# Weight pools kept open through all stages of a decoder trunk, and weight-block sums made by accumulating DMAs

## The chip, the cores and the metric

The kernel runs on one core of a Trainium2 chip. The core has five engines with in-order instruction queues of their own: TensorE (PE) for matmuls, VectorE (DVE), ScalarE (ACT), GpSimd (POOL) and SyncE (SP); PE also loads its stationary operand (PEld), which overlaps the matmuls. SP issues most DMAs, and POOL can issue them too; all of them run on the core's 16 DMA engines. Data live in HBM, in SBUF (128 partitions) and, for matmul results, in PSUM. The metric is the device time of one execution in microseconds (us); less is better.

## The reference

Two residual layers over 256 tokens of width 2048, in float32. Cut to what matters here:

```python
for layer in range(DEPTH):                                  # DEPTH = 2
    h = _rmsnorm(x, mix_norm_g[layer])
    if layer % 2 == 0:                                      # attention (8 heads) and a pooling mixer
        x = x + jnp.concatenate([a, b], axis=-1) @ even_w_out[e]
    else:                                                   # gated short convolution
        x = x + _short_conv(h, odd_w_in[o], odd_conv_w[o], odd_w_out[o])
    x = x + _mlp(_rmsnorm(x, mlp_norm_g[layer]), w_mlp_up[layer], w_mlp_down[layer])

def _mlp(h, w_up, w_down):                                  # 2048 -> 8192 -> 2048
    return jnp.square(jax.nn.relu(h @ w_up)) @ w_down
```

The weights are some 380 MB of float32, each read once per execution; the two MLPs hold most of them. The tokens are few, so nearly all of the work is weights passing through PE.

## The kernel before, in words

**Exactness.** PE multiplies in a reduced float32 form, so each operand is split: a high part `hi` (ACT casts it, line 140) and a low part `lo` (DVE subtracts, line 141). `halved` (line 131) does this for a weight tile of 1 MiB in two pieces, and each tile then gives PE two or three matmuls per block: `columns_out` (lines 157 to 161) where the weights are stationary, `tokens_out` (lines 146 to 155) where the tokens are, and `product` (lines 761 to 767) for blocks of the seven-product scheme below. A "tile" below is one such 1 MiB of weights, and its "preparation" the four instructions of `halved`.

**Weight pools.** `slab` (line 122) takes a buffer of the pool `raws`, issues its load on SP and calls `halved`, which takes buffers of the pool `halves` (six `hi` and six `lo`, three tiles' worth). `new_stage` (line 77) closes the pools of the stage that ends and opens new ones; it is called for the latents (line 213), after them (line 389), at the start of each MLP (line 715) and at the start of the convolution (line 898). In an MLP `raws` has two buffers and a pool `blocks` three, elsewhere `raws` has three.

**An MLP.** The hidden width 8192 is cut in 16 chunks of 512, and chunks go in eight pairs. `up_chunk(c)` makes one chunk's hidden values from four weight tiles (in four steps) and two steps of squaring and splitting. The product with `w_down` covers a pair's 1024 rows and 2048 columns in four column blocks of 512. Blocks 2 and 3 are done by `down_block`, two tiles each. For the first seven pairs blocks 0 and 1 are done by `down_seven` (line 750): the two token halves, the two column blocks and the pair's even and odd row groups make a 2 x 2 by 2 x 2 block product, which Strassen's scheme in Winograd's form does in seven products instead of eight. The token side of it (`sum_forms`, line 742) is made once per chunk. The weight side needs sums of the four blocks b11, b12, b21, b22 (rows even or odd, column block 0 or 1): DVE makes b12 - b11, b12 + b22, b22 + b11's new value and b21 - b22's new value, each in one instruction over 128 x 2048 elements (lines 787 and 790, called at 803, 812, 813 and 825). A running sum per product (`totals`) is kept over the pairs, and combined at the last of the seven. The last pair does all four blocks by `down_block`. The loop at lines 871 to 883 interleaves steps of `down_seven`, `up_chunk` and `down_block`.

**The order of the work.** A scheduler sorts each engine's instructions by its own estimate of when each could start; what waits for what is then kept by semaphores. So a change of the buffers can move instructions on engines that it does not name. At a stage's end the residual `x` gets its last column block (lines 858, 671 or 674, DVE), ACT squares it for the norm (`squares`, line 289), PE transposes it (`turn_block`, line 297) and ACT and DVE write the transposed block to `xT` (lines 204, 205). Since `xT` is filled block by block, the next stage's matmuls can begin before its last block is there.

## Time and profile before

| | us |
|---|---|
| median of 3 runs | 2035.02 |
| lowest and highest of them | 2035.01 and 2038.82 |
| the profiled execution's own time | 2038.12 |
| its span, first to last instruction | 2036.3 |
| PE busy | 2013.3 (99% of the span) |
| DVE busy | 1503.7 (74%) |
| ACT busy | 1115.8 (55%) |
| POOL busy | 52.5 (3%) |
| mean granted TensorE clock, share of 2.4 GHz | 0.997 |

PE's busy time is 99% of the span, so what is not PE's work is some 23 us in all. The chain of waits names the work that ended last, step by step; the waits of PE name each idle stretch and what ended it. The table of windows gives each engine's busy time in a stretch, the granted clock of TensorE as a share of 2.4 GHz, the mean busy share of the 16 DMA engines, and the rate at which they moved data. Matmuls are pipelined, so that the durations of single ones overlap, and what one costs is better taken from the chain's share divided by the count.

### The profile page before, as it was taken

The page shows a single profiled execution, that of the slowest core. Times are in us where ns is not written, and L with a number is a line of the kernel's source. Part 1 is how long each engine was busy: PE and PEld are TensorE (multiplying, and loading weights), DVE is VectorE, ACT ScalarE, POOL GpSimd, SP SyncE. Part 2 cuts the span into 40 slices and gives each one's busy share as a digit, 9 for nine tenths or more (in the row PEclk, how much of TensorE's full clock was granted, in tenths as well). Part 3 has the DMA queues.
Part 4 walks back from the last instruction along what each step waited for, and adds up shares of the span by engine and source line. Part 5 has one row for each costly group of instructions (what it writes and reads, how often), then busy time and mean ns, then how long its engine had stood idle before and what let it go on. Part 6 is the DMA issues. An engine that isn't in the chain of part 4 may idle for free.

```text
span 2036.3 us, 26507 instructions
## 1 busy us (share of the span) xinstructions
PE 2013.3 (99%) x10534; PEld 1726.1 (85%) x10534; DVE 1503.7 (74%) x1795; ACT 1115.8 (55%) x1480; POOL 52.5 (3%) x76
## 2 busy tenths in 40 slices
PE   8999999999999999999999999999999999999999
PEld 7987888888888888888788888888888888888887
DVE  5767559797887978875566656559797787978874
ACT  5457447565555655555444444546665556655552
POOL 2240000000000000000000000000000000000000
PEclk9999999999999999999999999999999999999999
DMA  7555365755757557555555555466665756657454
GB/s 243 160 173 182 128 197 178 225 176 191 230 165 231 166 187 227 166 182 183 173 186 186 186 186 187 164 216 197 196 200 171 241 167 203 206 166 239 154 186 145
DMA packets 195820, 384.20 MB, mean 189 GB/s; under 512 B 6224, under 2 KB 16336, under 8 KB 195696
## 3 DMA queue, kind: packets, MB, share of 16 engines
q1 hardware_dynamic: 195312, 382.23, 57.8%
q8 instruction: 82, 1.34, 0.3%
q0 software_dynamic: 352, 0.27, 0.1%
q14 instruction: 42, 0.34, 0.1%
q10 hardware_dynamic: 32, 0.01, 0.0%
HBM read 380.39 MB, written 2.10 MB: 188 GB/s over the span
## 4 chain that ended last, share of the span: by engine, by line
PE 97%; DMA 1%; ACT 1%; DVE 1%; issue 0%; SPq 0%; POOL 0%; DVEq 0%; ACTq 0%
PE ps L160 32%; PE ps L161 16%; PE ps L153 10%; PE ps L155 10%; PE ps L154 10%; PE ps L765 4%; PE ps L767 4%; PE ps L766 4%; PE ps L166 1%; PE ps L168 1%; PE ps L167 1%; DMA raw<-in_even_w_in 1%; PE ps L297 1%; ACT hi L140 0%; DVE lo L141 0%; PE ps L614 0%
## 5 line engine op out<-in xcount | busy, mean ns | idle before, releaser
L160 PE MATMUL ps<-xT,hi 128*128 128x512 f32 x2816 | 993.3, 395 | 3.3 <-ACT hi L140 3.3
L141 DVE TENSOR_TENSOR lo<-raw,hi 128x1024 fp32r<-128x1024 f32 (+2 forms) x610 | 739.3, 1226 | 331.5 <-ACT hi L140 327.9
L140 ACT CAST hi<-raw 128x1024 fp32r<-128x1024 f32 (+2 forms) x610 | 633.2, 1049 | 508.4 <-PE ps L160 206.5
L161 PE MATMUL ps<-xT,lo 128*128 128x256 f32 x2816 | 791.1, 281 | 0.2
L160 PEld LDWEIGHTS ps<-xT,hi 128*128 128x128 f32 x2816 | 530.5, 188 | 126.6 <-ACT hi L140 3.7
L161 PEld LDWEIGHTS ps<-xT,lo 128*128 128x128 f32 x2816 | 529.2, 188 | 5.3 <-DVE lo L141 1.4
L153 PE MATMUL ps<-hi,hT 128*128 128x512 f32 (+1 forms) x896 | 349.1, 390 | 0.0
L155 PE MATMUL ps<-hi,hT 128*128 128x512 f32 (+1 forms) x896 | 347.3, 388 | 0.0
L154 PE MATMUL ps<-lo,hT 128*128 128x512 f32 (+1 forms) x896 | 347.2, 387 | 0.0
L140 ACT CAST hi<-b 128x1024 fp32r<-128x1024 f32 x196 | 204.5, 1051 | 207.8 <-PE ps L160 161.6
L141 DVE TENSOR_TENSOR lo<-b,hi 128x1024 fp32r<-128x1024 f32 x196 | 237.6, 1220 | 44.9 <-ACT hi L140 44.6
L153 PEld LDWEIGHTS ps<-hi,hT 128*128 128x128 f32 x896 | 168.3, 188 | 35.0 <-issue 1.3
L155 PEld LDWEIGHTS ps<-hi,hT 128*128 128x128 f32 x896 | 168.3, 188 | 34.8
L154 PEld LDWEIGHTS ps<-lo,hT 128*128 128x128 f32 x896 | 168.3, 188 | 33.6 <-DVE lo L141 0.4
L765 PE MATMUL ps<-hi,fT 128*128 128x512 f32 x224 | 88.1, 393 | 0.0
L767 PE MATMUL ps<-hi,fT 128*128 128x512 f32 x224 | 87.7, 391 | 0.0
L766 PE MATMUL ps<-lo,fT 128*128 128x512 f32 x224 | 87.1, 389 | 0.0
L194 ACT COPY t<-ps 128x512 f32<-128x512 f32 x88 | 50.8, 578 | 53.6 <-PE ps L161 53.6
L858 DVE SCALAR_TENSOR_TENSOR x<-ps,r,x 128x512 f32<-128x512 f32 (+1 forms) x73 | 52.0, 739 | 19.3 <-PE ps L155 19.3
L765 PE MATMUL ps<-hi,hT 128*128 128x512 f32 x168 | 65.8, 392 | 0.2 <-ACT hT L200 0.2
L767 PE MATMUL ps<-hi,hT 128*128 128x512 f32 x168 | 65.6, 391 | 0.0
L766 PE MATMUL ps<-lo,hT 128*128 128x512 f32 x168 | 65.3, 389 | 0.0
(184 smaller groups left out, 1578.2 us busy)
## 6 DMA issues: line engine op xcount, KB each, us to landing
raw<-in_w_mlp_up SPq DMA_DIRECT2D x128, 1024.0 KB, 5.4
raw<-in_w_mlp_down SPq DMA_DIRECT2D x72, 1024.0 KB, 5.1
b<-in_w_mlp_down SPq DMA_DIRECT2D x56, 1024.0 KB, 6.0
raw<-in_odd_w_in SPq DMA_DIRECT2D x48, 1024.0 KB, 5.2
raw<-in_even_w_out SPq DMA_DIRECT2D x16, 1024.0 KB, 5.2
raw<-in_odd_w_out SPq DMA_DIRECT2D x16, 1024.0 KB, 5.3
raw<-in_even_w_in SPq DMA_DIRECT2D x8, 1024.0 KB, 5.7
raw<-in_even_w_in SPq DMA_DIRECT2D x7, 1088.0 KB, 6.5
```

The source lines that it names most:

```text
L140: a = nc.scalar.copy(h, r)
L141: v = nc.vector.tensor_tensor(out=l, in0=r, in1=h.bitcast(F32), op=ALU.subtract)
L153: nc.tensor.matmul(o, lhsT=a_hi, rhs=hi[:, c0:c0 + n], start=first, stop=False)
L154: nc.tensor.matmul(o, lhsT=a_hi, rhs=lo[:, c0:c0 + n], start=False, stop=False)
L155: nc.tensor.matmul(o, lhsT=a_lo, rhs=hi[:, c0:c0 + n], start=False, stop=last)
L160: nc.tensor.matmul(o, lhsT=hi[:, c0:c0 + P], rhs=act[:, kt, :], start=first, stop=False)
L161: nc.tensor.matmul(o[:, S:2 * S], lhsT=lo[:, c0:c0 + P], rhs=act[:, kt, 0:S], start=False, stop=last)
L194: nc.scalar.copy(t, ps[:, :, S:2 * S])
L765: nc.tensor.matmul(o, lhsT=a_hi, rhs=hi, start=q == 0, stop=False)
L766: nc.tensor.matmul(o, lhsT=a_hi, rhs=lo, start=False, stop=False)
L767: nc.tensor.matmul(o, lhsT=a_lo, rhs=hi, start=False, stop=q == 3)
L858: nc.vector.scalar_tensor_tensor(out=xb, in0=ps[:, t, :n], scalar=r2[0][:, t:t + 1], in1=xb, op0=ALU.mult, op1=ALU.add)
```

## The change

`new_stage` is split in two. With a value for `raw_bufs` it works as before. Without one it closes and opens only the pools named in `more`, and leaves `raws` and `halves` open: `raws` then keeps the three buffers it was given after the latents through both MLPs and the convolution. In an MLP `blocks` has one buffer of each of two tags, `t` and `v`.

`down_seven` no longer calls DVE for the weight side. The signs are chosen so that the four sums need additions alone (column block 0 enters with a negative sign, which the totals take back at the end): `t` is loaded with b12, b11 is added to it, later b22, later b21; `v` is loaded with b12 and b22 is added. Each addition is a DMA from HBM that accumulates into the SBUF tile, issued on POOL (`add`). Blocks b11, b22 and b21, which are used as they are, are loaded into `raws`. So a pair has five plain loads for its seven products where it had four, and four accumulating ones where it had four DVE instructions.

```diff
@@ -74,15 +74,16 @@
     big = ctx.enter_context(tc.tile_pool(name="big", bufs=1))
     stage = []
 
-    def new_stage(raw_bufs, **more):
-
-        for s_ in stage:
+    def new_stage(raw_bufs=0, **more):
+
+        for s_ in reversed(stage[1 - bool(raw_bufs):]):
             s_.close()
-        st = ExitStack()
-        stage[:] = [st]
-        pools.clear()
-        for name, bufs in dict(raws=raw_bufs, halves=6, **more).items():
-            pools[name] = st.enter_context(tc.tile_pool(name=uid(name), bufs=bufs, reuse_waits="tile"))
+        del stage[1 - bool(raw_bufs):]
+        for wanted in (dict(raws=raw_bufs, halves=6) if raw_bufs else {}, more):
+            if wanted:
+                stage.append(ExitStack())
+                for name, bufs in wanted.items():
+                    pools[name] = stage[-1].enter_context(tc.tile_pool(name=uid(name), bufs=bufs, reuse_waits="tile"))
 
     pools = {}
     small = ctx.enter_context(tc.tile_pool(name="small", bufs=2))
...
@@ -712,7 +713,7 @@
         up, down = w_up[layer], w_down[layer]
         hid, sums, totals = {}, {}, {}
         r2 = []
-        new_stage(2, blocks=3, forms=2)
+        new_stage(blocks=1, forms=2)
         pairs = DFF // NB // 2
 
         def up_chunk(c):
@@ -753,10 +754,16 @@
 
             rows_ = down[2 * pair * NB:2 * (pair + 1) * NB].rearrange("(q e p) n -> e p q n", e=2, p=P)
 
-            def block(e, n):
-                b = pools["blocks"].tile([P, 4, NB], F32, tag="b", name=uid("b"))
-                nc.sync.dma_start(b, rows_[e][:, :, n * NB:(n + 1) * NB])
+            def at(e, n):
+                return rows_[e][:, :, n * NB:(n + 1) * NB]
+
+            def block(e, n, tag="raw"):
+                b = pools["raws" if tag == "raw" else "blocks"].tile([P, 4, NB], F32, tag=tag, name=uid(tag))
+                nc.sync.dma_start(b, at(e, n))
                 return b
+
+            def add(b, e, n):
+                nc.gpsimd.dma_start(b, at(e, n), accum_op=ALU.add)
 
             def product(o, b, left):
 
@@ -795,46 +802,45 @@
 
             yield
             b11 = block(0, 0)
+            t = block(0, 1, "t")
+            add(t, 0, 0)
             one = bank2()
             product(one[:, 0, :], b11, own(0, 0))
             summed("p1", one[:, 0, :])
             yield
-            b12 = block(0, 1)
-            minus(b11, b12, b11)
-            product(one[:, 1, :], b11, form(1))
+            v = block(0, 1, "v")
+            add(v, 1, 1)
+            product(one[:, 1, :], t, form(1))
+            add(t, 1, 1)
             summed("p5", one[:, 1, :])
             yield
-            b22 = block(1, 1)
             two = bank2()
-            product(two[:, 0, :], b22, form(3))
+            product(two[:, 0, :], block(1, 1), form(3))
             onto(0, 1, two[:, 0, :])
             yield
-            plus(b12, b22, b12)
-            plus(b22, b22, b11)
-            product(two[:, 1, :], b22, form(2))
-            summed("p6", two[:, 1, :])
+            product(two[:, 1, :], v, form(0))
+            summed("p7", two[:, 1, :])
             yield
             three = bank2()
-            product(three[:, 0, :], b12, form(0))
-            summed("p7", three[:, 0, :])
+            product(three[:, 0, :], t, form(2))
+            add(t, 1, 0)
+            summed("p6", three[:, 0, :])
             yield
-            b21 = block(1, 0)
-            product(three[:, 1, :], b21, own(0, 1))
+            product(three[:, 1, :], block(1, 0), own(0, 1))
             onto(0, 0, three[:, 1, :])
             yield
-            minus(b22, b21, b22)
             four = bank2()
-            product(four[:, 0, :], b22, own(1, 1))
+            product(four[:, 0, :], t, own(1, 1))
             onto(1, 0, four[:, 0, :])
             if pair == pairs - 2:
                 onto(0, 0, totals["p1"])
-                plus(totals["p6"], totals["p6"], totals["p1"])
-                plus(totals["p7"], totals["p7"], totals["p6"])
-                onto(1, 0, totals["p7"])
-                plus(totals["p6"], totals["p6"], totals["p5"])
+                minus(totals["p1"], totals["p1"], totals["p6"])
+                minus(totals["p6"], totals["p5"], totals["p1"])
                 onto(0, 1, totals["p6"])
-                plus(totals["p7"], totals["p7"], totals["p5"])
-                onto(1, 1, totals["p7"])
+                minus(totals["p1"], totals["p1"], totals["p7"])
+                onto(1, 0, totals["p1"])
+                minus(totals["p5"], totals["p5"], totals["p1"])
+                onto(1, 1, totals["p5"])
 
         def down_block(pair, b, last):
 
@@ -895,7 +901,7 @@
     ss, xT = next_norm[0]
 
 
-    new_stage(3, conv=2)
+    new_stage(conv=2)
     conv_pool = pools["conv"]
     R1 = []
     yT = []
```

What the scheduler makes of it is seen in three places. The first is ACT's queue at the end of the first MLP and the start of the convolution; `hi<-raw_8452` in the kernel before and `hi<-raw_8450` in the changed one are the two halves of the convolution's first weight tile (`odd_w_in`), the `junk` rows the squares of a block of `x`, and the last `junk` pair is that of the last block. Before:

```order
L140 CAST hi_8403<-raw_8401 128x1024
L140 CAST hi_8407<-raw_8401 128x1024
L204 ACTIVATE xT_8195<-ps_8288,gains_577 128x256 x4
L289 ACTIVATE junk_8397,ss_8194<-x 128x512
L289 ACTIVATE junk_8399,ss_8194<-x 128x512
L204 ACTIVATE xT_8195<-ps_8380,gains_577 128x256 x4
L289 ACTIVATE junk_8511,ss_8194<-x 128x512
L289 ACTIVATE junk_8513,ss_8194<-x 128x512
L140 CAST hi_8454<-raw_8452 128x1024
L140 CAST hi_8458<-raw_8452 128x1024
```

And now:

```order
L141 CAST hi_8452<-raw_8450 128x1024
L205 ACTIVATE xT_8201<-ps_8294,gains_577 128x256
L141 CAST hi_8456<-raw_8450 128x1024
...
L290 ACTIVATE junk_8403,ss_8200<-x 128x512
L290 ACTIVATE junk_8405,ss_8200<-x 128x512
L141 CAST hi_8515<-raw_8513 128x1024
L141 CAST hi_8519<-raw_8513 128x1024
...
L290 ACTIVATE junk_8509,ss_8200<-x 128x512
L290 ACTIVATE junk_8511,ss_8200<-x 128x512
```

Three tiles of the convolution (6 casts) have moved ahead of the squares of the last block of `x`; before, all of them stood behind.

The second is PE's queue at the end of the attention layer's output projection and the start of the first MLP; `ident,x` are the transposes of the last block of `x`, the `xT,hi` rows the MLP's first tile. Before:

```order
L155 MATMUL ps_2602<-hi_2664,hT_1741 128x512
L160 MATMUL ps_2708<-xT_2333,hi_2712 128x512
L160 MATMUL ps_2709<-xT_2333,hi_2712 128x512
L297 MATMUL ps_2752<-ident,x 128x128 x8
L161 MATMUL ps_2708<-xT_2333,lo_2713 128x256
```

And now:

```order
L156 MATMUL ps_2602<-hi_2664,hT_1741 128x512
L161 MATMUL ps_2700<-xT_2333,hi_2704 128x512
L162 MATMUL ps_2700<-xT_2333,lo_2705 128x256
...
L161 MATMUL ps_2701<-xT_2333,hi_2708 128x512
L162 MATMUL ps_2701<-xT_2333,lo_2709 128x256
L298 MATMUL ps_2744<-ident,x 128x128 x8
```

The transposes stood behind two matmuls of the MLP, and now stand behind 32 (16 of each of the two lines). At the start of the second MLP they have moved back in the same way, by 30 matmuls.

The third is the DMA queues in the middle of the first MLP. SP's loads for one pair now, from the load of `t` on (`raw` with `w_mlp_up` are the tiles of `up_chunk`):

```order
L129 DMA raw_5123<-in_w_mlp_up 128x4x512
L762 DMA t_5270<-in_w_mlp_down 128x4x512
L129 DMA raw_5166<-in_w_mlp_down 128x4x512
L129 DMA raw_5232<-in_w_mlp_down 128x4x512
L762 DMA raw_5268<-in_w_mlp_down 128x4x512
L129 DMA raw_5297<-in_w_mlp_up 128x4x512
...
L129 DMA raw_5559<-in_w_mlp_down 128x4x512
L129 DMA raw_5625<-in_w_mlp_down 128x4x512
L762 DMA v_6050<-in_w_mlp_down 128x4x512
L762 DMA raw_5661<-in_w_mlp_down 128x4x512
```

And the additions on POOL, which had no instruction there before:

```order
L766 DMA t_5270<-in_w_mlp_down 128x4x512 x2
L766 DMA v_6050<-in_w_mlp_down 128x4x512
L766 DMA t_5270<-in_w_mlp_down 128x4x512
L766 DMA t_5981<-in_w_mlp_down 128x4x512 x2
L766 DMA v_6761<-in_w_mlp_down 128x4x512
```

The load of `t` stands three loads ahead of that of its pair's b11 (`raw_5268`), and the load and the addition of the next pair's `v` stand ahead of the third addition to this pair's `t`.

## Rows read from the trace of the kernel before

**Rows 1.** The page's busy time of each engine with the number of its instructions, and its costliest groups of matmuls (line, out<-in, count; then busy us, mean ns of one, idle us before).

```profile
PE 2013.3 (99%) x10534; PEld 1726.1 (85%) x10534; DVE 1503.7 (74%) x1795; ACT 1115.8 (55%) x1480; POOL 52.5 (3%) x76
...
L160 PE MATMUL ps<-xT,hi 128*128 128x512 f32 x2816 | 993.3, 395 | 3.3 <-ACT hi L140 3.3
...
L153 PE MATMUL ps<-hi,hT 128*128 128x512 f32 (+1 forms) x896 | 349.1, 390 | 0.0
...
L765 PE MATMUL ps<-hi,fT 128*128 128x512 f32 x224 | 88.1, 393 | 0.0
...
L765 PE MATMUL ps<-hi,hT 128*128 128x512 f32 x168 | 65.8, 392 | 0.2 <-ACT hT L200 0.2
```

**Rows 2.** The chain of waits, followed back from the last instruction: shares of the span by line.

```profile
by line: PE ps L160 31.9%; PE ps L161 16.2%; PE ps L153 10.4%; PE ps L155 10.3%; PE ps L154 10.3%; PE ps L765 4.4%; PE ps L767 4.4%; PE ps L766 4.3%; PE ps L166 0.8%; PE ps L168 0.8%; PE ps L167 0.8%; DMA raw<-in_even_w_in 0.7%; PE ps L297 
```

**Rows 3.** The waits of PE over the whole span: what waited, for what, us in total, times, longest.

```profile
PE ps L160 <- ACT hi L140: 3.3, 1, 3.3
PE ps L166 <- ACT qkv L521: 2.7, 1, 2.7
...
PE ps L297 <- DVE x L671: 0.9, 1, 0.9
PE ps L297 <- DVE x L674: 0.7, 2, 0.4
...
PE ps L765 <- ACT hT L200: 0.2, 1, 0.2
```

**Rows 4.** Windows over the first MLP, the second MLP from its first product on, and a stretch of 25 us in the first: start and end, us, then busy us and instructions of PE, PEld, DVE, ACT and POOL, granted clock, DMA share, GB/s.

```profile
282.00:972.00 690.00, 689.97 (x3521) 587.31 (x3520) 552.45 (x608) 399.90 (x486) 0.21 (x2) 1.00 0.61 195
1384.00:2033.00 649.00, 648.77 (x3297) 551.77 (x3295) 519.84 (x561) 366.10 (x429) 0.00 (x0) 1.00 0.59 190
575.00:600.00 25.00, 25.00 (x126) 21.18 (x125) 24.97 (x29) 14.31 (x18) 0.00 (x0) 1.00 0.29 87
```

**Rows 5.** PE in order of time at the end of the first MLP: start, us, instruction, idle before it and its releaser.

```profile
972.49 0.39 PE L155 MATMUL ps<-hi,hT 128*128 128x512 f32 x1
976.13 1.22 PE L160 MATMUL ps<-xT,hi 128*128 128x512 f32 x2 [3.25 <-ACT hi L140]
977.39 0.58 PE L161 MATMUL ps<-xT,lo 128*128 128x256 f32 x1
...
982.25 0.41 PE L161 MATMUL ps<-xT,lo 128*128 128x256 f32 x1
982.46 0.47 PE L160 MATMUL ps<-xT,hi 128*128 128x512 f32 x1
```

**Rows 6.** ACT in order of time at the same place, and at the end the residual's last column block on DVE.

```profile
970.51 0.47 ACT L204 ACTIVATE xT<-ps,gains 128x256 fp32r<-128x256 f32 x1 [0.55 <-DVE xT L205]
973.76 0.63 ACT L289 ACTIVATE junk<-x 128x512 f32<-128x512 f32 x1 [2.78 <-DVE x L858]
...
975.05 2.92 ACT L140 CAST hi<-raw 128x1024 fp32r<-128x1024 f32 x3
...
972.92 1.41 DVE L858 SCALAR_TENSOR_TENSOR x<-ps,r,x 128x512 f32<-128x512 f32 x2 [1.42 <-PE ps L155]
```

**Rows 7.** Windows there, the columns as in rows 4.

```profile
972.00:976.00 4.00, 0.88 (x4) 0.38 (x2) 2.13 (x7) 2.24 (x6) 0.38 (x1) 0.98 0.00 0
976.00:982.00 6.00, 5.83 (x17) 4.53 (x18) 6.00 (x8) 4.82 (x6) 0.32 (x1) 0.50 0.40 114
982.00:984.00 2.00, 2.00 (x12) 1.73 (x11) 1.01 (x1) 0.00 (x0) 0.00 (x0) 0.84 1.03 388
```

**Rows 8.** PE in order of time at the start of the second MLP.

```profile
1341.63 0.62 PE L160 MATMUL ps<-xT,hi 128*128 128x512 f32 x2
1342.64 0.33 PE L297 MATMUL ps<-ident,x 128*128 128x128 f32 x1 [0.39 <-DVE x L674]
1343.30 0.98 PE L297 MATMUL ps<-ident,x 128*128 128x128 f32 x7 [0.33 <-DVE x L674]
```

**Rows 9.** Instructions on the tile `b`: count, then min, median and max ns, first and last start.

```profile
L140 ACT CAST hi<-b x196: 1037/1052/1058, 316.3 to 1950.5; 128x1024 fp32r<-128x1024 f32 x196
L141 DVE TENSOR_TENSOR lo<-b,hi x196: 1210/1219/1227, 317.8 to 1951.8; 128x1024 fp32r<-128x1024 f32 x196
...
L790 DVE TENSOR_TENSOR b<-b,b x28: 2283/2290/2293, 320.2 to 1927.9; 128x2048 f32<-128x2048 f32 x28
L787 DVE TENSOR_TENSOR b<-b,b x28: 2280/2283/2291, 324.6 to 1917.7; 128x2048 f32<-128x2048 f32 x28
```

**Rows 10.** DMA issues by line: count, KB each, median us from issue to landing. The POOLq rows are from the kernel's start.

```profile
raw<-in_w_mlp_up SPq DMA_DIRECT2D x128, 1024.0 KB, 5.4
...
b<-in_w_mlp_down SPq DMA_DIRECT2D x56, 1024.0 KB, 6.0
...
qg<-in_even_q_norm_g POOLq DMA_DIRECT2D x1, 96.0 KB, 6.4
...
freq<-in_inv_freq POOLq DMA_DIRECT2D x1, 16.0 KB, 9.0
```

**Rows 11.** POOL's instructions by line: an addition of two 128 x 512 tiles, and a DMA issue; busy us, mean ns of one, idle before.

```profile
L485 POOL TENSOR_TENSOR pn<-pn 128x512 f32<-128x512 f32 x6 | 9.9, 1657 | 0.5
...
L232 POOL DMA_DIRECT2D rows<-in_mix_norm_g x1 | 0.7, 729 | 0.3 <-issue 0.3
```

More of the change, by code (lines that the diff above doesn't have):

```diff
@@ L211, in trunk @@
     ap_ = attn.enter_context(tc.tile_pool(name="attn", bufs=1, side="right"))
-    ctx.callback(lambda: stage[0].close())
+    ctx.callback(lambda: [s_.close() for s_ in reversed(stage)])
     new_stage(3)
```

## The prediction, made before the changed kernel ran

> **What bounds the kernel now.** I read the busy times first: PE is busy for 2013.3 of 2036.3 us, DVE for 74%, ACT for 55% and POOL for almost nothing [rows 1]. Next the chain of waits, which is PE's matmuls nearly end to end [rows 2]. So the time is PE's work plus PE's idle time, and a change that leaves the matmuls alone can win only idle time, or lose by making some. The third view, PE's waits, tells where the idle time is: the long ones are single events, with 3.3 us for `hi` at line 160, 2.7 us in the attention, 0.9 and 0.7 us for `x` before transposes, and 0.2 us at a seven-product matmul [rows 3]. The windows add what is missing: inside the MLPs, where the additions move, PE is busy for 689.97 of 690 us and 648.77 of 649 us, at the full 2.4 GHz, although DVE is at 24.97 of 25 us in places [rows 4]. A full DVE costs nothing there, because the preparation runs up to three tiles ahead of PE in the six pairs of `halves`.
>
> One place is different: the end of the first MLP. PE finishes the last down block at 972.9 and stands until 976.13 [rows 5]. ACT is idle meanwhile for 2.78 us, then squares the last block of `x`, and only behind that, at 975.05, casts the convolution's first tile [rows 6]. After the gap PE's clock is 0.50, which is 1.2 GHz, until 982.5 [rows 5, 7].
>
> **The change part by part.**
>
> *The additions leave DVE.* Two layers of seven pairs with four each: the 28 + 28 rows on `b`, 56 instructions of 2.29 us, 128 us of DVE [rows 9]. I cost this at nothing, since PE loses only 0.2 us to those products [rows 3, 4].
>
> *The pools stay open.* This moves instructions at three seams.
>
> (a) First MLP to convolution. Three tiles of casts now stand ahead of the last squares on ACT, into `halves` that PE has released long before. So PE has three tiles to go on with at 972.9, some 16 us by the price per tile below, and the 3.25 us go [rows 5]. With no gap I expect no fall of the clock either: 976.13 to 982.46 are 6.3 us at half speed, which hold 3.15 us of work at full speed, so 3.15 us go as well [rows 5, 7]. What is late next is the transposes of the last block, but they stand 32 matmuls behind the last down block, some 5 us, and DVE has `x` ready 1.4 us after it begins at 972.92 [rows 6].
>
> (b) Attention to first MLP: the transposes stand 30 matmuls later, some 5 us, so their wait of 0.9 us goes [rows 3].
>
> (c) Convolution to second MLP: the same, 0.7 us [rows 3, 8]. Together 3.25 + 3.15 + 0.9 + 0.7 = 8.0 us.
>
> *The additions as DMAs.* First how long a pair lasts. One `columns_out` costs 48.1% of 2036.3 us over 2816, 0.348 us; three `tokens_out` matmuls 31.0% over 896, 0.705 us; three of `product` 13.1% over 392, 0.680 us [rows 1, 2]. So an up tile (16) takes 5.57 us, a down tile (8) 5.64, a product (4) 2.72; a pair has 8, 4 and 7 of them, 86.2 us. It loads 16 MiB, 195 GB/s, as the window shows [rows 4].
>
> Two things must hold. *Latency:* the second addition to `t` can begin when `t`'s preparation for the second product is done, and is wanted three up tiles and two products later: 22.2 us at PE's pace. The third has two down tiles, a product and an up tile, 19.6 us. Beyond that PE has up to three prepared tiles, 8 to 17 us. On POOL's queue the next pair's `v` stands ahead of the third addition; its load comes behind the second down tile's on SP and waits for nothing that is late, so it holds up the third by a load of about 6 us at most [rows 10]. No row shows an accumulating DMA. Below, it can't land sooner than the plain load of that size, 5.4 to 6.0 us [rows 10]. Above, I add the longest landing of a POOL-issued DMA, 9.0 us for a mere 16 KB [rows 10], and POOL's own price for adding 1 MiB, 4 x 1.66 us [rows 11], to the plain load's: some 21 us. I take 12, between the plain load and half its upper price, since the transfer is the same 1 MiB; it is hidden, and even the upper end is but 2 us over the third's 19.6 and within what is prepared. POOL's issue, 0.7 us each, is on an idle engine [rows 11]. When the cover is gone, each addition costs its whole excess, on PE.
>
> *Throughput:* the pair's load grows from 16 to 17 plain MiB and four added ones, each worth c plain ones of DMA time. The engines move 388 GB/s when full, 2.70 us per MiB [rows 7]; by the MLP's mean share, 0.61 of 86.2 us for 16 MiB, it is 3.29 us [rows 4]. The DMAs fill 86.2 us at c = 3.7 by the first and c = 2.3 by the second. Below, c is 1; above, POOL's 6.6 us of adding on top of a plain 2.7 makes (2.7 + 6.6) / 2.7, about 3.4. I take 2, nearest the plain load but with a second operand read, so 25 MiB of plain load: 68 to 82 us of 86.2, full but not over.
>
> Two rules of the Trainium skill bear on this. *Collectives: The Full Stack* (section "The bandwidth ceiling: the fold count and why AG ≠ RS ≠ AR") has it that a reduction in the DMA engines runs at half the rate of a copy, not for the adding but for its second source read; by that c is 2 and the sum stays, while no run here shows it yet. *SBUF — State Buffer* (section "SBUF: two separate sides") speaks against the change: descriptors of a DMA issued from GpSimd are written by GpSimd itself, which a DVE instruction in its two-port mode locks out.
>
> The sum, against the profiled execution: 2038.12 - 8.0 = 2030.1 us. That execution stands 3.1 us above the median of 2035.02, about what one stretch at half clock costs, so the usual execution may have lacked one of the stretches. If it has the one at 976, it comes to 2035.02 - 8.0 = 2027.0; if it lacks that one, only the gaps go, 4.85 us, and it comes to 2030.2. I forecast the middle, 2028.5 us, with 2025 to 2031 as its own range.
>
> **The rivals.**
>
> *Less at the seams.* The transposes or the residual's last block could make a new gap of 1 to 3 us, or the fuller DMAs could bring the convolution's first tiles late. For it: DMA was at zero around 972 to 976 and is no longer [rows 7], and the loads of `t` and `v` go out in bursts. Against: order and buffers both favour PE. The saving is then 1 to 4 us: about 2032.5 us, no change that can be told.
>
> *The DMAs become the bound.* Place: every pair. Point from which it decides: c over 2.3 to 3.7. For it: the windows hold DMA shares over 1 for the plain loads alone when they come in a row [rows 7], and the stretch from a pair's down tiles to the next pair's b11 holds three of its four additions. Against: the rest of the pair, with most of its products, has room to catch up. Price at c = 4: 33 MiB x 2.70 = 89.1 us per pair, 2.9 us over, times 14 = 41 us, less the seams' 8: about 2068 us.
>
> *The adds wait for DVE.* DVE is at 24.97 of 25 us in places [rows 4]. If POOL could only make its descriptors when DVE stands idle, an addition could be 25 us late there; with 12 us of its own it would exceed the 19.6 us, and the prepared tiles, by perhaps 5 us in each pair, 70 us in all: about 2097 us. Against: the subtractions that fill DVE are 1.22 us each [rows 9], and a lock that ends with the instruction costs 1.2 us per addition, which is hidden. (This is the mechanism that the SBUF page's rule names; the instructions here are subtractions of two tiles.)
>
> *The change doesn't do what it says.* The order shows the additions on POOL and the casts moved, so I give it nothing.
>
> **How the numbers follow.** Chances: the forecast 0.56, less at the seams 0.20, the DMAs as a bound 0.20, the adds behind DVE 0.04. A measurement of this kernel can tell 0.2%, 4.1 us. Faster by more than that means under 2031.0: nearly all of the forecast, 0.55; within 0.2%: the second case and the forecast's edge, 0.21; slower: the last two, 0.24. For the range I leave out 3 in 100 below 2024.5, and above cut the DMA cases where they pass 2046, some 17 in 100.
>
> **What would show it right or wrong.** In the changed kernel's waits of PE the 3.3 us at the `odd_w_in` matmuls should be gone, as should those of the transposes for `x` at both MLPs' starts; the window after the seam should be at clock 1.00. In the MLPs PE should stay at over 99.9% busy, with a DMA share of 0.8 to 0.95, DVE lower by 64 us in each, and POOL's accumulating issues landing in 8 to 15 us. I am wrong if PE waits inside the MLPs for ACT's `hi<-t` or `hi<-v`, or for `hi<-raw` whose load is late; the first means latency, the second throughput. I am also wrong if the clock stays low after the first MLP without a gap before it.

## The result, and the profile after

The changed kernel takes 2026.65 us, the median of 4 runs (2025.33 to 2029.04); the kernel before took 2036.92 us beside it, the median of 4 (2035.01 to 2039.2). The ratio is 0.9949 with a 95% interval of 0.9934 to 0.9963: faster by 10.3 us, 0.5%. The forecast was 2028.5 us.

The line numbers have moved: L161 and L162 are now `columns_out`, L154 to L156 `tokens_out`, L772 to L774 `product`, and L766 is the additions. First the page: busy times, the two large DMA queues (packets, MB, share of 16 engines), POOL's issues of additions to `t` (busy us, mean ns), and DMA issues (count, KB, median us to landing).

```profile
PE 2005.9 (99%) x10534; PEld 1722.5 (85%) x10534; DVE 1389.5 (69%) x1739; ACT 1120.1 (55%) x1480; POOL 124.4 (6%) x132
...
q1 hardware_dynamic: 202704, 396.91, 58.5%
q0 software_dynamic: 29920, 59.00, 17.1%
...
L766 POOL DMA_DIRECT2D t<-in_w_mlp_down x42 | 54.4, 1296 | 1107.0 <-DVE lo L142 720.3
...
raw<-in_w_mlp_up SPq DMA_DIRECT2D x128, 1024.0 KB, 7.2
...
t<-in_w_mlp_down POOLq DMA_DIRECT2D x42, 1024.0 KB, 13.5
```

DVE is 114 us less busy with 56 instructions fewer than in [rows 1]; PE is 7.4 us less busy with the same 10534 matmuls. The accumulating queue (q0) took 17.1% for 59.00 MB and the plain one (q1) 58.5% for 396.91 MB: 0.290 against 0.147% per MB, so by these shares an accumulated MiB costs 1.97 plain ones. (The run without additions, below, gives a lower figure.)

The six longest waits of PE, which answer to [rows 3] (the others are 0.3 us and less), and windows over both MLPs and the end of the first, which answer to [rows 4, 7]:

```profile
PE ps L239 <- DMA rows<-in_mix_norm_g: 3.6, 1, 3.6
PE ps L167 <- ACT qkv L522: 3.0, 1, 3.0
PE ps L154 <- ACT xT L205: 2.9, 1, 2.9
PE ps L167 <- ACT hi L141: 1.9, 1, 1.9
PE ps L154 <- ACT hi L141: 1.9, 1, 1.9
PE ps L167 <- DVE hT L206: 0.4, 1, 0.4
```

```profile
971.00:976.00 5.00, 5.00 (x30) 4.35 (x29) 4.71 (x12) 3.67 (x7) 0.72 (x1) 1.00 0.25 73
976.00:982.00 6.00, 6.00 (x39) 5.37 (x38) 3.14 (x5) 3.35 (x5) 0.00 (x0) 1.00 0.71 232
282.00:972.00 690.00, 690.00 (x3522) 587.20 (x3521) 495.46 (x580) 402.53 (x485) 33.51 (x28) 1.00 0.83 242
1384.00:2020.00 636.00, 636.00 (x3230) 541.21 (x3228) 452.95 (x521) 358.89 (x415) 32.15 (x25) 1.00 0.85 244
```

The waits for `hi` at the convolution and for `x` at both MLPs are gone, and no wait of PE inside the MLPs has come; what is left belongs to the start and the attention. Behind the first MLP the granted clock is 1.00 where it was 0.50. The DMA share in the MLPs has risen from 0.61 and 0.59 to 0.83 and 0.85.

Where the 12.8 us between the two profiled spans (2036.3 and 2023.5) lie is read from the starts of the same matmuls in both: the transposes of the last block but one of `x` in the attention's output projection and in the first MLP, the first matmul of the convolution, the transposes behind it, and the first matmul of the second MLP. Two more places are shown for later, the 17th `xT,hi` matmul of each MLP, by which its transposes are done in both kernels. PE in order of time, before (976.13 and 1341.63 stand in [rows 5, 8]) and after:

```profile
273.24 1.03 PE L297 MATMUL ps<-ident,x 128*128 128x128 f32 x8
...
287.43 0.39 PE L160 MATMUL ps<-xT,hi 128*128 128x512 f32 x1
...
966.35 1.03 PE L297 MATMUL ps<-ident,x 128*128 128x128 f32 x8
...
985.00 1.04 PE L297 MATMUL ps<-ident,x 128*128 128x128 f32 x8
...
1349.65 0.39 PE L160 MATMUL ps<-xT,hi 128*128 128x512 f32 x1
```

```profile
272.68 1.03 PE L298 MATMUL ps<-ident,x 128*128 128x128 f32 x8
...
285.43 0.47 PE L161 MATMUL ps<-xT,hi 128*128 128x512 f32 x1
...
964.82 1.03 PE L298 MATMUL ps<-ident,x 128*128 128x128 f32 x8
...
970.96 0.39 PE L156 MATMUL ps<-hi,hT 128*128 128x512 f32 x1
971.18 0.40 PE L161 MATMUL ps<-xT,hi 128*128 128x512 f32 x1
...
976.77 1.04 PE L298 MATMUL ps<-ident,x 128*128 128x128 f32 x8
...
1330.32 0.40 PE L161 MATMUL ps<-xT,hi 128*128 128x512 f32 x1
...
1336.70 0.47 PE L161 MATMUL ps<-xT,hi 128*128 128x512 f32 x1
```

| stretch | lead at its end, us | won in it | forecast |
|---|---|---|---|
| start and attention | 0.56 | 0.56 | 0 |
| attention to first MLP, and the MLP | 1.53 | 0.97 | 0.9 |
| gap before the convolution | 4.95 | 3.42 | 3.25 |
| 16 pairs of matmuls behind it (half clock) | 8.23 | 3.28 | 3.15 |
| the rest of the convolution stage | 11.31 | 3.08 | 0 |
| second MLP | 12.8 | 1.5 | 0.7 |

The fifth row was not foreseen. There the clock is 1.00 and PE busy without a break in both kernels, and still it does more in the same time. Windows of 40 us in the convolution, before and then after (the second pair of numbers is PE's busy time and instructions):

```profile
1030.00:1070.00 40.00, 40.00 (x228) 34.85 (x227) 25.05 (x31) 16.85 (x18) 0.21 (x2) 1.00 0.57 187
```

```profile
1030.00:1070.00 40.00, 40.00 (x231) 35.06 (x230) 24.15 (x25) 17.93 (x20) 0.00 (x0) 1.00 0.56 185
```

By the starts in the trace, a pair of `columns_out` matmuls follows the last every 353.4 ns before and every 348.9 ns after. A run of pairs keeps one pace until other matmuls, transposes or products, interrupt it. Before, 748 pairs of the convolution have the slow pace (702 of them behind the transposes for the norm, L317), 3.3 us in all; after, 46 there and 110 at the start of each MLP, 1.2 us.

### The profile page after: what moved, and what is told of

Read it like the earlier page. It is cut to its first block, busy times and chain, and to the rows that moved or that the text cites. A ratio compares the mean times of both kernels' runs of the same rounds, so it can differ in the third digit from the quotient of the medians.

```text
span 2023.5 us, 26714 instructions
## 1 busy us (share of the span) xinstructions
PE 2005.9 (99%) x10534; PEld 1722.5 (85%) x10534; DVE 1389.5 (69%) x1739; ACT 1120.1 (55%) x1480; POOL 124.4 (6%) x132
## 3 DMA queue, kind: packets, MB, share of 16 engines
q1 hardware_dynamic: 202704, 396.91, 58.5%
q0 software_dynamic: 29920, 59.00, 17.1%
## 4 chain that ended last, share of the span: by engine, by line
PE 98%; DMA 1%; ACT 1%; SPq 0%; issue 0%; DVE 0%; ACTq 0%
PE ps L161 32%; PE ps L162 16%; PE ps L154 11%; PE ps L155 11%; PE ps L156 11%; PE ps L772 4%; PE ps L774 4%; PE ps L773 4%; PE ps L167 1%; PE ps L168 1%; PE ps L169 1%; PE ps L298 1%; DMA raw<-in_even_w_in 1%; PE ps L615 0%; ACT hi L141 0%; PE ps L619 0%
## 5 line engine op out<-in xcount | busy, mean ns | idle before, releaser
L142 DVE TENSOR_TENSOR lo<-raw,hi 128x1024 fp32r<-128x1024 f32 (+2 forms) x694 | 847.8, 1227 | 413.9 <-ACT hi L141 409.6
L141 ACT CAST hi<-raw 128x1024 fp32r<-128x1024 f32 (+2 forms) x694 | 724.8, 1049 | 620.9 <-PE ps L161 285.2
L161 PE MATMUL ps<-xT,hi 128*128 128x512 f32 x2816 | 988.9, 394 | 0.0
L162 PE MATMUL ps<-xT,lo 128*128 128x256 f32 x2816 | 789.5, 280 | 0.0
L161 PEld LDWEIGHTS ps<-xT,hi 128*128 128x128 f32 x2816 | 529.5, 188 | 122.1
L162 PEld LDWEIGHTS ps<-xT,lo 128*128 128x128 f32 x2816 | 527.6, 187 | 3.7
L154 PE MATMUL ps<-hi,hT 128*128 128x512 f32 (+1 forms) x896 | 349.1, 390 | 0.0
L156 PE MATMUL ps<-hi,hT 128*128 128x512 f32 (+1 forms) x896 | 347.3, 388 | 0.0
L154 PEld LDWEIGHTS ps<-hi,hT 128*128 128x128 f32 x896 | 168.3, 188 | 35.1 <-issue 1.3
L156 PEld LDWEIGHTS ps<-hi,hT 128*128 128x128 f32 x896 | 168.2, 188 | 34.7
L142 DVE TENSOR_TENSOR lo<-t,hi 128x1024 fp32r<-128x1024 f32 x84 | 102.6, 1221 | 45.2 <-ACT hi L141 45.1
L141 ACT CAST hi<-t 128x1024 fp32r<-128x1024 f32 x84 | 87.3, 1051 | 73.2 <-PE ps L161 50.7
L766 POOL DMA_DIRECT2D t<-in_w_mlp_down x42 | 54.4, 1296 | 1107.0 <-DVE lo L142 720.3
L772 PE MATMUL ps<-hi,fT 128*128 128x512 f32 x224 | 88.1, 393 | 0.0
L774 PE MATMUL ps<-hi,fT 128*128 128x512 f32 x224 | 87.7, 391 | 0.0
L772 PE MATMUL ps<-hi,hT 128*128 128x512 f32 x168 | 65.8, 392 | 0.0
L774 PE MATMUL ps<-hi,hT 128*128 128x512 f32 x168 | 65.6, 391 | 0.0
## 6 DMA issues: line engine op xcount, KB each, us to landing
t<-in_w_mlp_down POOLq DMA_DIRECT2D x42, 1024.0 KB, 13.5
```

Source lines behind the costliest of these rows:

```text
L141: a = nc.scalar.copy(h, r)
L142: v = nc.vector.tensor_tensor(out=l, in0=r, in1=h.bitcast(F32), op=ALU.subtract)
L154: nc.tensor.matmul(o, lhsT=a_hi, rhs=hi[:, c0:c0 + n], start=first, stop=False)
L156: nc.tensor.matmul(o, lhsT=a_lo, rhs=hi[:, c0:c0 + n], start=False, stop=last)
L161: nc.tensor.matmul(o, lhsT=hi[:, c0:c0 + P], rhs=act[:, kt, :], start=first, stop=False)
L162: nc.tensor.matmul(o[:, S:2 * S], lhsT=lo[:, c0:c0 + P], rhs=act[:, kt, 0:S], start=False, stop=last)
```

## The experiments

Two theories. *Seams*: the time comes from PE's gaps, the half clock behind one of them, and the pace; the additions cost and bring nothing. *VectorE*: it comes from the 114 us that left DVE. Each ratio is to the kernel before, run beside it.

**A second look at both kernels.** No edit.

> The kernel before, unchanged, for a second profile. In the first one the pairs of matmuls of `columns_out` follow each other every 353.4 ns for 750 pairs of the convolution (from 985.8 to 1250 us), and every 349.0 ns in both MLPs; the changed kernel has 353.4 ns in only 268 pairs. That is 2.1 us of the difference between the two profiles, and the prediction had no term for it. If the program sets the pitch, the same 750 pairs have 353.4 ns again. If it is chance, some of them have 349.0 ns, and the time of the execution is up to 3.3 us shorter. The gap of 3.25 us after the first MLP and the clock at 0.50 behind it should be there again in either case.

> The changed kernel, unchanged, on the chip of the next three runs and for a second profile. 2026 to 2030 us. By both theories the waits for `hi` and for `x` at the seams are absent again and the clock behind the first MLP is 1.00. If the program sets the pitch of the pairs of matmuls, the pairs behind the transposes at both MLPs' starts and at the convolution's start (110, 46 and 110) come every 353.4 ns again, and the 702 of the convolution behind them every 348.9 ns.

Measured: before 2039.35 us in the profiled execution; after 2026.99 us (5 runs), ratio 0.9949, 0.9936 to 0.9961. The gap of 3.25 us is there again in the one and absent in the other. The paces are the same place by place in both pairs of profiles, so the program sets them, not chance. The half clock behind the gap, 6.3 us long in the first profile [rows 5, 7], is shorter here; first the gap in PE's order of time, then windows behind it:

```profile
974.69 0.39 PE L155 MATMUL ps<-hi,hT 128*128 128x512 f32 x1
978.33 0.79 PE L160 MATMUL ps<-xT,hi 128*128 128x512 f32 x2 [3.25 <-ACT hi L140]
```

```profile
979.00:983.00 4.00, 3.53 (x14) 3.04 (x14) 4.00 (x5) 4.00 (x5) 0.00 (x0) 0.59 0.26 55
983.00:986.00 3.00, 3.00 (x19) 2.59 (x18) 2.20 (x2) 0.01 (x1) 0.00 (x0) 1.00 1.03 389
```

A mean clock of 0.59 is half clock for 3.3 of the 4 us. So this term is 3.3 us in the first pair of profiles; in this one, by the starts of the same matmuls, it is 2.2 us.

**Pools alone.** DVE makes the sums; `raws` keeps the two buffers of an MLP through the convolution.

```diff
-        new_stage(2, blocks=3, forms=2)
+        new_stage(*(() if layer else (2,)), blocks=3, forms=2)
...
-    new_stage(3, conv=2)
+    new_stage(conv=2)
```

> The kernel before, its sums of blocks on VectorE as they were, but the pools `raws` (two buffers) and `halves` opened at the first MLP and left open to the end. Theory (the gain is PE's idle and slow time at the seams): the gap of 3.25 us before the convolution and the half clock behind it go, and the 0.7 us before the second MLP, while the 0.9 us before the first MLP stay: 7.1 us, and up to 3 us more if the convolution's pairs come at 349 ns; 2027 to 2030 us, with VectorE as busy as before, some 1504 us. Rival (the gain is VectorE's 114 us): as before, 2035 to 2039 us.

Measured: 2029.1 us, ratio 0.9954, 0.9941 to 0.9966. The page and the waits of PE:

```profile
PE 2008.6 (99%) x10534; PEld 1725.0 (85%) x10534; DVE 1503.9 (74%) x1795; ACT 1116.2 (55%) x1480; POOL 52.7 (3%) x76
...
PE ps L298 <- DVE x L672: 0.9, 1, 0.9
```

DVE is as busy as before and the gain is there, though this version keeps the wait of 0.9 us; by its interval it can't be told from the changed kernel. The *VectorE* theory falls.

**One order put back.** In the changed kernel, the convolution's first casts are held behind the last squares.

```diff
-                a = nc.scalar.copy(h, r)
+                with behind(*hold):
+                    a = nc.scalar.copy(h, r)
...
         if not R1:
+            hold.append(squares(ss, 3))
+        pss = gate(1)
+        hold.clear()
```

> The changed kernel with one order put back: the casts of the convolution's first weight tiles stand behind the squares of the last block of `x` on ScalarE, as in the kernel before; pools and DMAs stay. Theory (the gap brings the half clock): PE waits some 3.3 us before the convolution, runs at 0.50 for some 6 us after it, and the time rises by 3.25 + 3.15 = 6.4 us, to 2033 us, by up to 3 us more or less with the pitch of the convolution's pairs. Rival (the half clock had another cause): the gap alone, 3.3 us, 2030 us, and a granted clock of 1.00. Rival (the seam does not matter): 2026 to 2028 us.

Measured: 2034.99 us (11 runs), ratio 0.9983, 0.9974 to 0.9992, so 0.0034 or 6.9 us above the changed kernel's ratio; 6.4 were expected. PE in order of time, and a window behind:

```profile
971.86 0.39 PE L157 MATMUL ps<-hi,hT 128*128 128x512 f32 x1
975.50 0.76 PE L162 MATMUL ps<-xT,hi 128*128 128x512 f32 x2 [3.25 <-ACT hi L142]
```

```profile
976.00:982.00 6.00, 6.00 (x29) 5.42 (x28) 6.00 (x6) 4.18 (x5) 0.00 (x0) 0.72 0.52 161
```

One order on ACT brings back the gap, and with it the clock below full behind it, with pools and DMAs untouched. In this profile, of the fastest of the 11 executions, the two take 3.4 and 1.8 us by the starts of the same matmuls. This is the largest term of the prediction, shown alone.

**The additions alone.** Pools closed and opened at each stage as before, two buffers of `raws` in the MLPs.

```diff
-        new_stage(blocks=1, forms=2)
+        new_stage(2, blocks=1, forms=2)
...
-    new_stage(conv=2)
+    new_stage(3, conv=2)
```

> The accumulating DMAs as in the changed kernel, but every stage closes all pools and opens new ones as before, with two buffers in `raws` in the MLPs and three in the convolution; the casts of the convolution's first tile stand behind the last squares on ScalarE again. Theory (seams): the gap of some 3.3 us before the convolution, the half clock and the waits for `x` at both MLPs are back: 2033 to 2039 us although VectorE is some 114 us less busy. Rival (VectorE): 2025 to 2029 us. A third outcome: with five plain loads for a pair's products in two buffers, PE waits for loads inside the MLPs, and the time is over 2040 us.

Measured: 2154.99 us, ratio 1.0573, 1.0556 to 1.0589: the third outcome. The waits show why, two lines of ACT's first, then two of PE's:

```profile
ACT hi L140 <- DMA raw<-in_w_mlp_up: 310.1, 72, 10.7
...
ACT hi L140 <- DMA raw<-in_w_mlp_down: 252.3, 80, 9.4
...
PE ps L160 <- ACT hi L140: 24.3, 16, 3.3
PE ps L771 <- DVE p L793: 20.7, 12, 2.1
```

ACT waits 562 us for weight loads, and PE runs out of prepared tiles again and again. The next run asks whether the missing buffer or the additions did it.

**The same with three buffers.** As above, with `new_stage(3, blocks=1, forms=2)`.

> The changed kernel's DMAs with three buffers in `raws` everywhere, but every stage closes all pools and opens new ones. In its order the casts of the convolution's first tile stand ahead of the last squares, and the transposes for `x` stand behind two matmuls at all three seams, as they did before at two. Theory A (the gain comes from what stands where in the queues at the seams): only the waits for `x` come back, 0.9, 0.7 and about 1 us at the convolution, without a fall of the clock: 2.6 us over the changed kernel, 2029 to 2031 us; inside the MLPs PE waits for nothing, since the third buffer is there, and so the 115 us that the kernel with additions and two buffers lost were the missing buffer. Theory B (pools that live on are needed as such): a gap of 3 us at the convolution with the half clock, 2033 us or more. Theory C (the additions themselves were too late in the kernel with two buffers): 2100 us or more here too.

Measured: 2031.36 us, ratio 0.9973, 0.9963 to 0.9984. Theory A holds by the waits, which are those for `x`, and no clock falls at the convolution's start; the time lies just above its 2029 to 2031 us.

```profile
PE ps L297 <- DVE x L671: 0.9, 1, 0.9
PE ps L297 <- DVE x L863: 0.7, 2, 0.4
PE ps L297 <- DVE x L674: 0.7, 2, 0.4
```

```profile
973.00:977.00 4.00, 3.29 (x16) 2.31 (x15) 2.33 (x4) 3.11 (x6) 0.00 (x0) 1.00 0.00 0
```

It is 4.4 us over the changed kernel run beside it, where 2.6 were expected. The two profiled executions, 2034.92 and 2027.92 us, are 7.0 apart. By the starts of the same matmuls 2.2 us of that are the slow pace, which 762 pairs have here against 266, and 4.8 us lie at the three seams (1.5, 1.7 and 1.6), although the waits there add up to 2.3 us only. Why the medians lie closer than the profiled executions is open. Some 124 us of the run before (2154.99 against 2031.36) were the third buffer: three of a pair's five plain loads of blocks now pass through `raws`.

**No additions.** `add` does nothing.

> The changed kernel without its 56 accumulating DMAs: `t` and `v` hold one block each where they should hold sums, so the additions are left out of the computation. Theory (they are hidden): the time of the changed kernel within 1.5 us, and the DMA share in the MLPs falls from 0.83 to 17/25 of it, 0.57. Rival (they cost PE something that the list of waits does not show, as slower matmuls beside full DMAs): over 2 us faster than the changed kernel, under 2025 us.

Measured: 2027.11 us, ratio 0.9948, 0.9935 to 0.9960, against 2026.99 for the changed kernel beside it. The plain loads' queue, and the first MLP's window, with the DMA share at 0.64 where 0.57 was expected:

```profile
q1 hardware_dynamic: 202704, 396.91, 61.2%
...
282.00:965.00 683.00, 683.00 (x3489) 581.36 (x3488) 493.79 (x575) 402.24 (x485) 0.21 (x2) 1.00 0.64 202
```

The additions cost no time that can be seen. The share fell less than expected because the plain loads took 61.2% here for the same bytes that took 58.5% beside the additions. So the price of an addition depends on how it is read: both queues together took 75.6% of 2023.5 us with the additions and 61.3% of 2025.3 without, 288 us more for 56 additions, or 5.1 us each. A plain MiB took 3.27 us here, so by the difference c is 1.6, not 1.97.

**Five copies per pair.** Behind each load of a block:

```diff
+                        nc.sync.dma_start(spare[r:r + P, :], up[0:P, 0:2048])
```

> The changed kernel with five more DMAs of 1 MiB per pair, from HBM to HBM, each issued on SyncE behind one of the five loads of blocks; nobody waits for them. It asks how far the DMAs are from being the bound. The accumulating DMAs took 1.97 times the engines' time of plain loads per byte, so a pair's 17 + 4 x 1.97 = 24.9 loads fill 0.83 of 85.7 us, 2.86 us per MiB. If a copy costs what a plain load costs, the share goes to 0.83 x 29.9 / 24.9 = 1.00, and the time rises by little: 2030 to 2070 us, with PE waiting for casts that wait for loads. If a copy costs two loads, the share would be 1.16, a pair 99 us and the time 2027 + 14 x 14 = some 2220 us. Rival (there is far more room than the share tells): 2026 to 2030 us.

Measured: 2064.14 us, ratio 1.0128, 1.0113 to 1.0144. Queue q1 took 65.8% of 2066.7 us here and 58.6% of 2026.1 us in the changed kernel, 173 us more for 70 copies: 2.5 us each, 0.79 of a load's 3.1 us. So a pair has 28.8 plain loads' worth, where it had 24.9, with 1.97 for an addition (27.2 and 23.3 with 1.6).

```profile
PE ps L779 <- DVE p L801: 22.7, 12, 2.1
...
282.00:965.00 683.00, 669.53 (x3396) 566.70 (x3395) 475.74 (x558) 381.89 (x462) 33.64 (x28) 1.00 0.93 288
...
583.50 2.00 ACT L141 CAST hi<-raw 128x1024 fp32r<-128x1024 f32 x2 [9.13 <-DMA raw<-in_w_mlp_down]
...
603.18 0.47 PE L779 MATMUL ps<-hi,fT 128*128 128x512 f32 x1 [1.65 <-DVE p L801]
```

The lines are PE's waits, the first MLP's window, and ACT and PE in order of time in one pair. PE waits some 2 us at a product, nearly once in each pair. The releaser named is a running sum on DVE; 20 us earlier ACT had stood 9.13 us for a late load, and both engines were still catching up. Around that load the DMA share is over 1:

```profile
575.00:580.00 5.00, 5.00 (x31) 4.35 (x30) 0.81 (x1) 0.00 (x0) 0.00 (x0) 1.00 1.10 258
580.00:585.00 5.00, 5.00 (x27) 4.26 (x26) 0.41 (x1) 1.50 (x2) 0.00 (x0) 1.00 1.07 341
```

So at a mean share of 0.93 loads already come late. That bursts fill the engines before the mean does is read from these two windows; no run tests it apart.

**Two more additions in a row.** `add(t, 1, 1)` three times.

> The changed kernel with the second addition to `t` made three times, one behind the other, so six accumulating DMAs in a pair instead of four; two of a block too many are in `t`, so the sums are not the reference's. It asks how much latency the second addition has left, beside the DMA load. The load is 17 + 6 x 1.97 = 28.8 plain loads per pair, the same as with five copies (17 + 4 x 1.97 + 5 x 0.79 = 28.8), which took 2064 us. Latency: three additions in a row at the median landing of 13.5 us are 41 us, against the 22.2 us of slack and 8 to 17 us of prepared tiles that the prediction worked out: 2 to 11 us late in each pair, with PE waiting for `hi` of `t` at the fifth product. Theory (both count): over 2064 us, 2075 to 2200. Rival (only the load counts): 2055 to 2070 us. Rival (neither, the additions have more room than worked out): under 2045 us.

Measured: 2183.5 us, ratio 1.0705, 1.0686 to 1.0725. By the same count the DMA load is that of the copies (28.8), but the place is another:

```profile
PE ps L772 <- ACT hi L141: 107.6, 14, 9.5
...
ACT hi L141 <- DMA t<-in_w_mlp_down: 269.2, 14, 20.6
```

Once in each pair PE waits 7.7 us for `t`, within the 2 to 11 us worked out. PE is also 42 us longer busy than in the changed kernel's second profile, with a mean clock of 0.966 over the span. Latency is a limit of its own, and lies where the slack said.

**The pace.** The last transpose of `x` repeated (two runs, with different counts).

```diff
+        again = {"mlp": 1 + 2 * i, "mix1": 2}.get(which, 0)
...
+                for _ in range(1 + (again if (b, k, t) == (3, 3, T - 1) else 0)):
```

> The changed kernel with the last of the eight transposes of the last block of `x` repeated: once at the first MLP, twice at the convolution, three times at the second MLP. It asks what sets the pace of the pairs of matmuls behind the transposes, which come every 353.4 ns in all three places in the changed kernel (110, 46 and 110 pairs) and every 349.0 ns elsewhere. If the number of transposes in between sets it, at least one of the three places turns to 349.0 ns. If the place in the program does, all three stay. The time tells nothing here: the repeats cost some 0.5 us and the three places hold 1.2 us.

> The changed kernel with the last of the eight transposes of the last block of `x` made three times at both MLPs' starts, so ten in a row there; at the convolution there are eight as before. In the run before this one ten in a row at the convolution turned the pace of the 46 pairs behind them from 353.4 to 348.9 ns, and that of the 701 behind the next interruption from 348.9 to 353.3, while nine and eleven at the MLPs left 353.3. If the number of transposes sets the pace, both MLPs' 110 pairs turn to 349.0 ns here and the convolution stays as in the changed kernel (46 at 353.4, 702 at 348.9): 1.0 us less, against some 0.4 us for the four transposes; 2026.4 us, which can't be told from the changed kernel's 2026.65 and 2026.99 us by its time. If the place sets it, the MLPs keep 353.4 ns and the time rises by 0.4 us.

Measured, ns per pair:

| | first MLP, 110 | convolution, 46 | convolution, 701 | second MLP, 110 |
|---|---|---|---|---|
| changed kernel (8, 8, 8 transposes) | 353.4 | 353.4 | 348.9 | 353.4 |
| 9, 10, 11 | 353.3 | 348.9 | 353.3 | 353.3 |
| 10, 8, 10 | 348.9 | 353.4 | 353.3 | 348.9 |

The first of the two took 2032.03 us (one run), the second 2029.2 us (ratio 0.9954, 0.9941 to 0.9968). Ten in a row give 348.9 ns at all three places, so the place does not set the pace. But the 701 pairs turned slow in the last row although nothing near them changed, which was not expected (2026.4 us was the forecast for this version), so the local count is not all of it either. Of the 2.2 us that this version lost against 2026.99, the pace is 701 x 4.4 ns less 220 x 4.4 ns, 2.1 us. No version here beat the changed kernel.

## Why the prediction was right, and where it was not

*The gap and the clock (a)* were right in place, cause and size: 3.42 and 3.28 us in the first pair of profiles against 3.25 and 3.15, and 3.4 and 2.2 in the second. Putting one order on ACT back returned both. The doubt about which executions have the half clock was in place too, only it is not there or absent, but longer or shorter.

*The waits for `x` (b, c)* are gone as worked out, but their price was too low, and that 0.97 us stands against 0.9 in the table is luck. From an MLP's first matmul to its 17th `xT,hi` the lead grew by 1.44 us in the first MLP (0.56 to 2.00) and by 1.64 in the second (11.31 to 12.95), where the idle time was 0.9 and 0.7. So each place cost 0.5 to 0.9 us more than PE's idle time there; why is not shown. The slow pace at the MLPs' starts then took 0.5 us back in each, and at the second MLP's first products another 0.5 us was won that is not explained further.

*The additions at nothing* was right: 2026.99 with them and 2027.11 without. The terms behind it held in the main. The factor c, taken as 2, is 1.97 by the shares of one profile and 1.6 by the difference that the additions make. The rule of the Trainium skill (*Collectives: The Full Stack*, section "The bandwidth ceiling: the fold count and why AG ≠ RS ≠ AR"), a reduction at half the rate of a copy, which the page measured on rings of cores, agrees with the first number and not with the second. Landing, taken as 12 us, is 13.5 for `t`, with the bounds at 5.4 and 21. The share, forecast as 0.8 to 0.95, is 0.83 to 0.85. POOL's issue was under-sized: 1.30 us (54.4 us for 42) where 0.7 stood, on an idle engine.

*DVE's relief at nothing* was right too: pools alone bring the gain. The relief itself was 114 us, where 128 was forecast.

*The step that failed* is the opening one: "a change that leaves the matmuls alone can win only idle time". PE's busy time fell by 7.4 us with the same matmuls. 3.3 of it is the clock, which the prediction itself counted in spite of that sentence; the pace of the pairs is net 2.1 (3.3 us before, 1.2 after); 1.5 is what the two waits for `x` cost beyond their idle time; the last 0.5 is not traced further. The prediction took one price for `columns_out`, 0.348 us, from a sum over stages, and so passed over the convolution's 353.4 ns. The profiled pair, from which the terms are read, differs by 12.8 us: the 8.0 that were summed, 2.1 of pace, 1.5 at the waits, 0.56 ahead of the first MLP and some 0.5 at the second MLP's first products. The medians differ by 10.3, because the profiled execution lay 1.2 us above its median before and 1.3 below it after. That the forecast lay only 1.9 us too high, although 4.8 us of the profiled pair's gain were missing from its sum, is in part luck.

*The rivals.* "Less at the seams" did not come: the first tiles were prepared in time. "The DMAs become the bound" did not come at this c, but its point was about right: between 24.9 loads' worth per pair, which cost nothing, and 28.8, which cost 37 us, the bound sets in. The latter would be c = 2.95 for four additions (2.6 with the lower price of an addition), within the 2.3 to 3.7 named. "The adds wait for DVE" did not come: no wait of PE on `t` or `v`. What it rested on, DVE at 24.97 of 25 us, is gone with the additions themselves, so the lock that the Trainium skill names (*SBUF — State Buffer*, section "SBUF: two separate sides") is neither shown nor refuted here. "The change doesn't do what it says" fell with POOL's 56 issues.

What the prediction did not see is how its two parts hang together. The additions free DVE, which was worth nothing, but they also send three blocks of a pair through `raws`; with two buffers there, as before, that costs some 124 us. The third buffer makes the additions free, and it does so whether the pools stay open or are opened anew with three.

## What to carry to other kernels

When one engine is 99% busy, look at stage seams for what stands in front of its first operands on the feeding engines: a few instructions in the wrong order cost a gap of 3.3 us here, and the clock behind it another 2 to 3.3. A resource that is 60% busy on average can take a good deal of work at no cost, but the room ends before 100%, and by a burst or a latency at one place; work out slack in both. Take the price of a matmul stage by stage, not from the sum.

## What was not expected of the hardware

The same pairs of matmuls, at the same granted clock and with PE never idle, run at one of two paces, 348.9 or 353.4 ns, each for hundreds of pairs. It changes only where other matmuls (transposes or products) come between, is the same in a second profile of the same program, and at the seams it depends on the number of transposes there and on something earlier. What carries it is open. It is worth up to 3.3 us here, as much as the gap that the change removed.

A wait of PE for `x` cost more than its idle time: 1.44 and 1.64 us where 0.9 and 0.7 were idle.

The half clock behind the same gap of 3.25 us lasted 6.3 us in one execution and some 3.3 in another, and waits of 0.7 and 0.9 us brought none. An accumulating DMA of 1 MiB into SBUF took the engines 1.97 times a plain load by the shares of one profile and 1.6 times by the difference to a run without additions; a copy from HBM to HBM took 0.79 times, by the difference of its queue.
